# The opening of a hybrid decoder layer on one core: low parts written over their sums, a common ring of nine tiles, and the first weights split in halves

## The chip, the core and the metric

The kernel runs on one core of one Trainium2 chip. The metric is the device time of one execution in microseconds; lower is better. The core has four engines that compute (TensorE or PE, VectorE or DVE, ScalarE or ACT, GpSimd or POOL) and SyncE (SP), whose queue issues all of this kernel's DMAs. The engines run side by side and wait for one another through semaphores; each works through its own queue in order.

## What is computed

One decoder layer with two attention branches over the same input. The reference, cut to what matters:

```python
xn = rms_norm(h, norm_gain[l])                    # 16 meta tokens + 2048 tokens, 1024 wide
proj = xn @ w_in[l]                               # 1024 -> 6400 columns
sb_q, sb_k, sb_v, sw_q, sw_k, sw_v, sb_z, sw_z, g_sb, g_sw = jnp.split(proj, offsets, axis=-1)
o_sb = stick_breaking_attention(sb_q, sb_k, sb_v)          # 8 heads of 64
o_sw = sliding_window_sink_attention(rope(sw_q), rope(sw_k), sw_v, sinks)   # 16 heads, 2 k/v heads
y_sb = (o_sb * jax.nn.silu(sb_z)) @ w_branch_sb[l]
y_sw = (o_sw * jax.nn.silu(sw_z)) @ w_branch_swa[l]
merged = jax.nn.sigmoid(g_sb) * y_sb + jax.nn.sigmoid(g_sw) * y_sw
h = h + merged @ w_out[l]
return rms_norm(h, final_norm_gain)[:, BLOCK:]
```

All of it is float32. The kernel gets that accuracy by splitting each operand in a high part (`fp32r`) and a low part (what the high part leaves), and by making three products of each pair: high by high, low by high, high by low. A *split* is therefore everywhere: ScalarE writes the high part, and VectorE or GpSimd writes source minus high part.

## The kernel before

**Tiling.** Tokens lie in four groups of 512; groups 2 and 3 (`g0`, `g1` in the code of the opening) are the first half, groups 0 and 1 the second. A *column tile* is 128 columns of `w_in` for one group: 8 slices of the 1024-long contraction, three matmuls each, 24 matmuls of 128x512 (lines 402, 403, 404: xh by wh, xl by wh, xh by wl). Where the meta tokens are wanted too, 16 small matmuls of 128 columns follow (line 413, `gemm_meta`).

**The opening** (pool "start", lines 945 to 1046) begins before the norms are known. Three column tiles are wanted first: the keys of stick-breaking head pair 0 (`sb_k(0)`), the queries (`sb_q(0)`) and the keys of pair 1 (`sb_k(1)`). For both groups they are multiplied on x times gain alone (`unscaled`, lines 914 to 919), and the six sums are multiplied by the row scales afterwards (`scaled`, line 941: VectorE takes a sum from PSUM into a `tmp` tile). The sums are then split (`evac_split`, lines 112 to 114) and written to DRAM (`kd`, `qd`). Meanwhile x is normalised for good (`normal`, lines 373 to 378: VectorE multiplies by gain and scale, line 375; ScalarE writes the high part xh, line 376; VectorE writes the low part xl, line 378), first for g0, then for g1. `in_turns` does two slices at a time.

**After it** come, in this order on TensorE: the window branch's k, v and first q tile for g0 (banks g, g, z), k for g1 (bank o), v for g1 (bank z), its second q tile for g0, the stick-breaking v tile `sb_v(0)` for g1 and then g0. Rope (lines 597 to 603) takes four ScalarE copies, two VectorE operations and a GpSimd addition; `put_k` (lines 605 to 613) writes four casts and four differences into `kk`.

**Work that hangs behind a tile** is kept in three lists, `soon`, `late` and `pending`. `lagged` empties them at the third, fifth and seventh of a column tile's slices, so TensorE's order has a tile's transposes (lines 425, 471, 510, 521, 537) inside the next tile.

**Turned v.** `sb_v` makes differences of neighbouring tokens of v, and `rows` turns them: four transposes into the single bank zm (line 510), then a split into a tile `vt` of 128 x 4 x 2 x 128, which lies in the weights' `raw` buffers for g < 2 and in a buffer of its own otherwise, and one DMA per tile of v.

**Buffers.** The ring `tmp` has 7 tiles of 128x512 floats; the weights have 3 buffers each for wh and wl and 2 for `raw`; `xs` has 4. Banks in PSUM: g 2, z 2, t 2, zm 1, o 1. A buffer is free again when all that read it are done, DMAs to DRAM included.

**What sets the order.** TensorE's queue is in the order in which the code is written. ScalarE's and SyncE's queues are in written order inside the pool "start", VectorE's up to `hand.close()`; everywhere else a scheduler places instructions by a simulated time line when the program is built. The spills of split weights to DRAM (kept for the other group) are put in a list, `put_off`, in the opening.

## Time and profile before

| what | value |
|---|---|
| time, median of 3 runs | 2190.73 us (2188.23 to 2192.26) |
| time of the profiled execution | 2189.51 us |
| its span, first to last instruction | 2187.8 us |
| TensorE busy | 2153.3 us, 98% |
| VectorE busy | 1357.2 us, 62% |
| ScalarE busy | 1007.7 us, 46% |
| GpSimd busy | 370.6 us, 17% |
| mean granted clock of TensorE | 0.996 |

In a timeline row the columns are: start in us from the span's start, duration in us, engine, line, operation, what is written and what is read, shapes, the number of like instructions merged in the row, and in brackets the engine's idle time just before with the instruction that ended it. A matmul's duration has its pipeline in it, so the pace of a stream is read from the distance between starts. PE is the matmul, PEld its weight load, SPq SyncE's DMA queue. In the table by stages the columns are: the stage, its length, busy time and number of instructions for each engine, the granted clock (1.00 is full speed), the busy share of the DMA engines and GB/s.

### The profile page before, as it was taken

The numbers are of one execution on the slowest core, as the hardware profiler recorded it, in microseconds if no ns is written. First come the engines' busy times: TensorE is split into PE (matmuls) and PEld (weight loads), VectorE is DVE, ScalarE is ACT, GpSimd is POOL, SyncE is SP. The second block draws the span as 40 slices with busy tenths as digits, with TensorE's granted clock in tenths as the row PEclk, the third lists the DMA queues.
The fourth block names the chain that finished last, engine by engine and source line by source line (L and its number), as shares of the span: only waits on it lengthen the run. The fifth ranks groups of instructions, "written<-read, shape, count | busy, mean of one in ns | idle before, by whom it ended". The sixth has DMA issues, their size and how long they took to land.

```text
span 2187.8 us, 30234 instructions
## 1 busy us (share of the span) xinstructions
PE 2153.3 (98%) x10614; PEld 1768.4 (81%) x10614; DVE 1357.2 (62%) x2117; ACT 1007.7 (46%) x2327; POOL 370.6 (17%) x485
## 2 busy tenths in 40 slices
PE   8899999999999999999999999999999999999998
PEld 6678888888888888888887888888888888787886
DVE  6678776355555443777755888788774436454453
ACT  6566766244444423767753555555553301221121
POOL 1123333322322200222310000000000232000000
PEclk9899999999999999999999999999999999999999
DMA  9655544856565365444446433323323985468422
GB/s 336 236 174 182 176 174 168 275 191 199 185 194 186 125 220 164 155 154 147 143 162 190 121 111 114 113 98 114 119 86 107 353 290 189 167 221 280 154 97 87
DMA packets 174648, 380.41 MB, mean 174 GB/s; under 512 B 22912, under 2 KB 41088, under 8 KB 174496
## 3 DMA queue, kind: packets, MB, share of 16 engines
q1 hardware_dynamic: 174496, 378.48, 51.6%
q8 instruction: 84, 1.38, 0.3%
q14 instruction: 68, 0.56, 0.1%
HBM read 237.35 MB, written 140.98 MB: 173 GB/s over the span
## 4 chain that ended last, share of the span: by engine, by line
PE 88%; DVE 2%; issue 2%; ACT 2%; DMA 1%; POOL 0%; POOLq 0%; SPq 0%; ACTq 0%; DVEq 0%
PE ps_g L402 15%; PE ps_g L403 14%; PE ps_g L404 14%; PE ps_o L868 6%; PE ps_z L820 6%; PE ps_t L842 5%; PE ps_o L723 2%; PE ps_z L677 2%; PE ps_g L225 1%; PE ps_g L226 1%; PE ps_z L226 1%; PE ps_g L224 1%; PE ps_z L224 1%; PE ps_z L225 1%; PE ps_t L226 1%
## 5 line engine op out<-in xcount | busy, mean ns | idle before, releaser
L402 PE MATMUL ps_g<-xh,wh 128*128 128x512 f32 x1544 | 638.9, 414 | 7.9 <-ACT xh L918 7.5
L403 PE MATMUL ps_g<-xl,wh 128*128 128x512 f32 x1544 | 607.9, 394 | 0.5 <-DVE xl L919 0.5
L404 PE MATMUL ps_g<-xh,wl 128*128 128x512 f32 x1544 | 608.0, 394 | 0.0
L831 DVE TENSOR_TENSOR_SCAN row<-row 128x512 f32<-128x512 f32 (+2 forms) x320 | 371.2, 1162 | 167.9 <-POOL row L829 97.0
L404 PEld LDWEIGHTS ps_g<-xh,wl 128*128 128x128 f32 x1544 | 291.0, 188 | 65.6
L402 PEld LDWEIGHTS ps_g<-xh,wh 128*128 128x128 f32 x1544 | 292.5, 189 | 55.3 <-ACT xh L918 7.5
L403 PEld LDWEIGHTS ps_g<-xl,wh 128*128 128x128 f32 x1544 | 292.9, 190 | 44.1 <-DVE xl L919 1.0
L824 ACT ACTIVATE row<-ps_z 128x512 f32<-128x512 f32 (+1 forms) x320 | 171.9, 538 | 253.0 <-PE ps_z L820 208.8
L114 DVE SCALAR_TENSOR_TENSOR wtl<-ps_t,wth 128x512 fp32r<-128x512 f32 (+1 forms) x320 | 190.0, 594 | 46.7 <-ACT wth L113 45.2
L113 ACT ACTIVATE wth<-ps_t 128x512 fp32r<-128x512 f32 (+1 forms) x320 | 170.2, 532 | 91.4 <-PE ps_t L842 89.5
L820 PE MATMUL ps_z<-kt,q 128*128 128x512 f32 (+3 forms) x640 | 185.0, 369 | 0.3 <-ACT row L824 0.3
L842 PE MATMUL ps_t<-ident,row 128*128 128x128 f32 x1088 | 171.6, 273 | 1.2 <-DVE row L831 1.2
L842 PEld LDWEIGHTS ps_t<-ident,row 128*128 128x128 f32 x1088 | 135.9, 140 | 37.3 <-DVE row L831 1.7
L829 POOL TENSOR_SCALAR_AFFINE_SELECT row<-row 128x128 f32<-128x128 f32 x128 | 44.9, 352 | 620.1 <-ACT row L824 548.0
L820 PEld LDWEIGHTS ps_z<-kt,q 128*128 128x128 f32 x640 | 118.7, 188 | 26.4 <-ACT row L824 0.8
L109 POOL TENSOR_SCALAR wh<-raw 128x1024 fp32r<-128x1024 f32 (+1 forms) x63 | 66.7, 1059 | 357.6 <-PE ps_g L403 217.6
L868 PE MATMUL ps_o<-wth,vc 128*128 128x512 f32 (+1 forms) x320 | 125.7, 393 | 1.2 <-DVE tmp L873 1.1
L553 ACT ACTIVATE tmp<-ps_g 128x512 f32<-128x512 f32 x112 | 67.0, 598 | 117.5 <-PE ps_g L404 111.1
L868 PE MATMUL ps_o<-wtl,vc 128*128 128x512 f32 (+1 forms) x320 | 116.8, 365 | 0.0
L685 ACT ACTIVATE sc<-sc,nm 128x129 f32<-128x129 f32 x256 | 100.0, 393 | 36.1 <-DVE nm L683 35.4
L110 POOL TENSOR_TENSOR wl<-raw,wh 128x1024 fp32r<-128x1024 f32 (+1 forms) x43 | 95.8, 2228 | 3.2
L603 POOL TENSOR_TENSOR tmp<-tmp 128x512 f32<-128x512 f32 (+1 forms) x37 | 47.7, 1290 | 195.3 <-DMA qd<-tmp 72.2
(302 smaller groups left out, 3412.7 us busy)
## 6 DMA issues: line engine op xcount, KB each, us to landing
wh<-h_in_w_in SPq DMA_DIRECT2D x66, 512.0 KB, 4.0
wl<-l_in_w_in SPq DMA_DIRECT2D x66, 512.0 KB, 4.7
raw<-in_w_in SPq DMA_DIRECT2D x50, 512.0 KB, 5.7
h_in_w_in<-wh SPq DMA_DIRECT2D x50, 512.0 KB, 3.3
l_in_w_in<-wl SPq DMA_DIRECT2D x50, 512.0 KB, 2.9
q<-qd SPq DMA_DIRECT2D x128, 128.0 KB, 2.9
vc<-vd SPq DMA_DIRECT2D x48, 256.0 KB, 3.3
kd<-tmp SPq DMA_DIRECT2D x32, 256.0 KB, 3.8
```

What stands on the lines that cost most here:

```text
L110: (V if vsplit[0] else G).tensor_tensor(l, src, f32(h), op=ALU.subtract)
L113: A.activation(h, acc, AF.Copy, scale=scale)
L114: V.scalar_tensor_tensor(l, acc, scale, f32(h), op0=ALU.mult, op1=ALU.subtract)
L402: T.matmul(acc, lhsT=wh[:, k, :], rhs=xh[g][:, k, :], start=k == 0, stop=False)
L403: T.matmul(acc, lhsT=wh[:, k, :], rhs=xl[g][:, k, :], start=False, stop=False)
L404: T.matmul(acc, lhsT=wl[:, k, :], rhs=xh[g][:, k, :], start=False, stop=k == KT - 1)
L685: A.activation(sc[:, hh, :], sc[:, hh, :], AF.Exp, bias=nm[:, hh:hh + 1], accum_out=den[:, hh:hh + 1])
L820: T.matmul(z[:, :w], lhsT=lq, rhs=kt[h][:, k0:k0 + w], start=t == 0, stop=t == 1)
L824: A.activation(r[:, :w], z[:, :w], AF.Sigmoid, scale=-1.0)
L831: V.tensor_tensor_scan(r[:, :w], r[:, :w], r[:, :w], last[j] if n else 1.0, op0=ALU.mult, op1=ALU.min)
L842: T.transpose(tr[:, j * P:(j + 1) * P], rows_of[h, g, n - (j > i), j][:, k0:k0 + P], ident)
L868: T.matmul(o[:, :n], lhsT=v, rhs=r, start=first and r is wh, stop=last and r is wl)
```

## The change

Eight edits, all but two in the opening:

- **First weights in halves.** The weights of `sb_k(0)` are loaded first, then the gains, then x; the identity matrix is loaded later. The split is made in halves along the contraction (`by_halves`): ScalarE casts the first four slices, VectorE makes their low part; after the first slice of x, ScalarE casts the other four, and GpSimd makes their low part.
- **Low parts over sums.** In the opening `low(acc)` gives the sum's own tile as the place for its low part, so a split takes one new `tmp` tile and not two.
- **The second group's splits come earlier.** The sums of g1 are scaled and split inside the opening, before g1 is normalised; before, they were split after three column tiles.
- **Spills later.** The spills in `put_off` and the two parked sums are issued behind the splits' DMAs, the spills behind the last two loads of x.
- **The ring has 9 tiles** (7 before).
- **Turned v goes through the ring:** each tile is split in two halves (`a` = 0, 1), each 128 x 4 x 128 in a `tmp` tile, with a DMA each. The `vt` buffers go.
- **Parked sums.** The meta sums of the two key tiles come back from DRAM into the scales' tile `rb` (named `back`), both at once and earlier; the work that reads them is flushed one tile later than before. The transposed meta keys of the window branch use bank t.
- **Keys and queries held.** `put_k` and the q tile's splits for g0 are held (`then`, `waiting`) until all of the rope work of that stretch stands in VectorE's queue; `put_k` of g1 is held until the turn of v is flushed.

The core of the diff:

```diff
-        return tp.tile([rows, GT], dt, tag="tmp", name="tmp", bufs=7)
+        return tp.tile([rows, GT], dt, tag="tmp", name="tmp", bufs=9)
...
+    spare = [False]
+    def low(acc):
+        return acc.bitcast(F32R) if spare[0] else tmp(F32R)
+    sums_back = []
     def sb_k(p):
         def use(g, acc, ms):
-            h, l = tmp(F32R), tmp(F32R)
+            h, l = tmp(F32R), low(acc)
...
-                    if p < 2:
-                        t = tp.tile([NM, P], F32, tag="ms", name="ms", bufs=2)
-                        DMA(t, msd[p])
-                    mc = meta_cols(t if p < 2 else ms, "t" if p < 2 else "zm")
+                    mc = meta_cols(sums_back[p] if p < 2 else ms, "t" if p < 2 else "zm")
...
     def sb_q(p):
-            h, l = tmp(F32R), tmp(F32R)
+            h, l = tmp(F32R), low(acc)
...
-                if g < 2:
-                    vt = wp.tile([P, 4, 2, P], F32R, tag="raw", name="vt", bufs=2)
-                else:
-                    vt = tp.tile([P, 4, 2, P], F32R, tag="vt", name="vt", bufs=1)
-                evac_split(vt[:, :, :, 0:64], vt[:, :, :, 64:128], tr.rearrange("p (b a d) -> p b a d", b=4, a=2))
-                DMA(vd[p][g].rearrange("a p b d -> p b a d"), vt)
+                hl = tr.rearrange("p (b a d) -> p a b d", b=4, a=2)
+                for a in range(2):
+                    vt = tmp(F32R).rearrange("p (b d) -> p b d", b=4)
+                    evac_split(vt[:, :, 0:64], vt[:, :, 64:128], hl[:, a])
+                    DMA(vd[p][g][a], vt)
...
+    waiting = []
+    def then(f):
+        if hold[0]:
+            waiting.append(f)
+        else:
+            f()
+    hold = [False]
...
-                put_k(t, n * GT, GT)
+                then(lambda: put_k(t, n * GT, GT))
...
+        def by_halves(wh, wl, raw):
+            a, b = slice(0, KT // 2), slice(KT // 2, KT)
+            A.copy(wh[:, a], raw[:, a])
+            V.tensor_tensor(wl[:, a], raw[:, a], f32(wh[:, a]), op=ALU.subtract)
+            def rest():
+                A.copy(wh[:, b], raw[:, b])
+                G.tensor_tensor(wl[:, b], raw[:, b], f32(wh[:, b]), op=ALU.subtract)
+            second.append(rest)
+        raw = load(C_SBK)
+        DMA(gn, gain.rearrange("o (k p) -> p (o k)", p=P))
+        ready[C_SBK] = weights(C_SBK, raw=raw, split=by_halves)
...
             unscaled(g0, k, raws[k])
+            if k == 0:
+                second[0]()
         ts.append(sbt[2]())
+        DMA(ident, ident_c)
...
-        for n in (0, 2):
-            DMA(msd[n // 2], ms[n])
-        for k, t in put_off:
-            DMA(k, t)
-        del put_off[:]
         ready[C_SWQ] = weights(C_SWQ, raw=raw)
+        spare[0] = True
         outs[g0, 2] = scaled(g0, 2, rb0)
         for n in range(3):
             ts[n][1](g0, outs[g0, n], ms[n])
         for n in range(3):
             outs[g1, n] = scaled(g1, n, rb1)
-        for k, t in put_off:
-            DMA(k, t)
+        for n in range(3):
+            ts[n][1](g1, outs[g1, n], None)
+        spare[0] = False
+        for n in (0, 2):
+            DMA(msd[n // 2], ms[n])
         for k in range(0, KT, 2):
             in_turns(*(normal(g1, j, new[j], rb1) for j in (k, k + 1)))
             if k == 0:
                 for j in (6, 7):
                     new.append(ring_x())
                     DMA(new[j], xt[g1, j])
+                for j, t in put_off:
+                    DMA(j, t)
...
+                hold[0] = True
                 drain(col_tile(wk, g0, use_k), col_tile(wv, g0, use_v), col_tile(wq, g0, use_q, bank="z"))
-                for n in range(3):
-                    ts[n][1](g1, outs[g1, n], None)
+                flush(waiting)
                 drain(lagged(col_tile(wk, g1, use_k, True, "o", "t")))
+                hold[0] = False
                 meta_k = pending[:]
                 del pending[:]
                 drain(col_tile(wv, g1, use_v, True, "z", "t"))
+                pending.append(lambda: flush(waiting))
+                back = tp.tile([P, GT], F32, tag="rb", name="back", bufs=1)
+                for i in range(2):
+                    sums_back.append(back[:NM, i * P:(i + 1) * P])
+                    DMA(sums_back[i], msd[i])
...
-                pending.extend(held)
+                pending.append(lambda: pending.extend(held))
```

What this does to the queues is seen at three places. TensorE's own order stays as it was, but for three small transposes.

The first is VectorE's queue where the six sums are scaled and split. `tmp<-ps` is a sum being scaled, `tmp<-tmp` the low part of a split, `xs<-xs,gn,rb` and `raw<-raw,gn,rb` slices of x for g1 being normalised, `xl` their low parts. Before:

```order
L941 TENSOR_TENSOR tmp<-ps_z,rb_529 128x512
L114 SCALAR_TENSOR_TENSOR tmp<-tmp 128x512 x3
L941 TENSOR_TENSOR tmp<-ps_z,rb 128x512
L941 TENSOR_TENSOR tmp<-ps_o,rb 128x512
L941 TENSOR_TENSOR tmp<-ps_t,rb 128x512
L375 SCALAR_TENSOR_TENSOR xs<-xs,gn,rb 128x512 x2
L378 TENSOR_TENSOR xl<-xs,xh 128x512 x2
```

The change:

```order
L957 TENSOR_TENSOR tmp<-ps_z,rb_531 128x512
L112 SCALAR_TENSOR_TENSOR tmp<-tmp 128x512 x3
L957 TENSOR_TENSOR tmp<-ps_z,rb 128x512
L957 TENSOR_TENSOR tmp<-ps_o,rb 128x512
L957 TENSOR_TENSOR tmp<-ps_t,rb 128x512
L112 SCALAR_TENSOR_TENSOR tmp<-tmp 128x512 x3
L373 SCALAR_TENSOR_TENSOR xs<-xs,gn,rb 128x512 x2
L376 TENSOR_TENSOR xl<-xs,xh 128x512 x2
```

Three more low parts stand ahead of the normalised x; before, those three stood some fifteen rows further down.

The second place is SyncE's queue at the same point: `h_in_w_in` and `l_in_w_in` are spills of weights, `msd` the parked sums, `ct` and `sn` the rope tables, `kd` and `qd` the split sums, `xs<-in_xt` the last two slices of x for g1. Before:

```order
L55 DMA raw<-in_xt 128x512 x2
L55 DMA msd_289<-ms 16x128
L55 DMA msd_290<-ms 16x128
L55 DMA h_in_w_in_641<-wh 128x1024
L55 DMA l_in_w_in_642<-wl 128x1024
L55 DMA h_in_w_in_658<-wh 128x1024
L55 DMA l_in_w_in_659<-wl 128x1024
L55 DMA kd_2_98<-tmp 128x512 x2
L55 DMA qd_2_82<-tmp 128x512 x2
L55 DMA kd_2_102<-tmp 128x512 x2
```

The change, from the same load on:

```order
L55 DMA raw<-in_xt 128x512 x2
L55 DMA kd_2_96<-tmp 128x512 x2
L55 DMA qd_2_80<-tmp 128x512 x2
L55 DMA kd_2_100<-tmp 128x512 x2
L55 DMA ct<-in_cost 128x1024
L55 DMA sn<-in_sint 128x1024
```

and some rows on, behind the second group's split sums:

```order
L55 DMA msd_287<-ms 16x128
L55 DMA msd_288<-ms 16x128
L55 DMA xs<-in_xt 128x512 x2
L55 DMA h_in_w_in_643<-wh 128x1024
L55 DMA l_in_w_in_644<-wl 128x1024
```

Four spills of 512 KB each no longer stand ahead of the first split sums; all six stand behind the last slices of x.

The third place is the start of ScalarE's queue. Before:

```order
L65 ACT_TABLE_LOAD
L107 CAST wh<-raw 128x1024
L918 ACTIVATE xh<-raw_322,gn 128x512
L918 ACTIVATE xh<-raw_326,gn 128x512
L918 ACTIVATE xh<-raw_330,gn 128x512
```

The change:

```order
L65 ACT_TABLE_LOAD
L972 CAST wh<-raw 128x512
L934 ACTIVATE xh<-raw_321,gn 128x512
L976 CAST wh<-raw 128x512
L934 ACTIVATE xh<-raw_327,gn 128x512
```

Half of the cast now stands behind the first slice of x, and the low part of that half has moved from VectorE's queue to GpSimd's.

More of the change, by code (lines that the diff above doesn't have):

```diff
@@ L66, in tile_kernel @@
     ident = cp.tile([P, P], F32, name="ident")
-    DMA(ident, ident_c)
     gn = cp.tile([P, KT], F32, name="gn")
-    DMA(gn, gain.rearrange("o (k p) -> p (o k)", p=P))
     sel = cp.tile([P, 2, P], I32, name="sel")
@@ L163, in load, with weights @@
         return raw
-    def weights(c0, w=w_in, raw=None):
+    def weights(c0, w=w_in, raw=None, split=split):
         if c0 in ready:
@@ L626, in later @@
                         t, u = (tmp()[:, :NM] for _ in range(2))
-                        rope(meta_cols(ms), cm, sm, t, u, 1.0)
+                        rope(meta_cols(ms, "t"), cm, sm, t, u, 1.0)
                         put_k(t, 8 * P, NM)
@@ L654, in use, with put_q @@
                 q = sp.tile([P, 2, GT], F32R, tag="q", name="q", bufs=QB)
-                for a in range(2):
-                    r = slice(64 * a, 64 * a + 64)
-                    o = slice(64 - 64 * a, 128 - 64 * a)
-                    A.copy(q[r, a, :], t[r])
-                    V.tensor_tensor(q[o, a, :], t[r], f32(q[r, a, :]), op=ALU.subtract)
+                def put_q():
+                    for a in range(2):
+                        r = slice(64 * a, 64 * a + 64)
+                        o = slice(64 - 64 * a, 128 - 64 * a)
+                        A.copy(q[r, a, :], t[r])
+                        V.tensor_tensor(q[o, a, :], t[r], f32(q[r, a, :]), op=ALU.subtract)
+                then(put_q)
                 qs[p, g] = q, clock[0] + QW
@@ L951, in tile_kernel @@
             V.memset(t, 0.0)
+        second = []
+        def by_halves(wh, wl, raw):
[9 more added lines that the diff above has]
+        ready[C_SBK] = weights(C_SBK, raw=raw, split=by_halves)
         ts = [sbt[0]()]
```

## The prediction, made before the changed kernel was run

> **What bounds the kernel now.** I read the page first: the span, the busy shares and the chain of work that ended last, then its list of DMA issues.

> ```profile
> span 2187.8 us, 30234 instructions
> PE 88%; DVE 2%; issue 2%; ACT 2%; DMA 1%; POOL 0%; POOLq 0%; SPq 0%; ACTq 0%; DVEq 0%
> kd<-tmp SPq DMA_DIRECT2D x32, 256.0 KB, 3.8
> ```

> TensorE carries 88% of the chain, so a change that leaves its work alone can win only where it waits or runs at a lower clock. A table by stages shows where.

> ```profile
> 7.46:13.62 6.16, 5.65 (x13) 4.08 (x14) 5.88 (x9) 4.94 (x8) 0.00 (x0) 1.00 1.03 366
> 13.62:63.85 50.23, 50.23 (x246) 41.17 (x245) 33.59 (x64) 29.36 (x62) 8.02 (x10) 1.00 0.96 357
> 63.85:78.98 15.13, 10.25 (x45) 6.70 (x44) 12.56 (x15) 7.25 (x12) 5.38 (x3) 0.89 0.77 260
> 78.98:107.54 28.56, 23.08 (x115) 18.44 (x113) 20.04 (x36) 18.05 (x39) 5.21 (x6) 0.86 0.58 200
> 107.54:114.23 6.69, 6.69 (x27) 5.24 (x26) 0.56 (x4) 0.63 (x3) 0.00 (x0) 0.85 0.00 0
> 114.23:165.00 50.77, 47.69 (x258) 39.60 (x257) 41.07 (x79) 34.95 (x102) 14.08 (x17) 1.00 0.56 187
> 165.00:2187.80 2022.80, 2009.70 (x9922) 1653.14 (x9920) 1241.52 (x1909) 909.52 (x2100) 335.50 (x441) 1.00 0.50 168
> ```

> After 165 us it is busy for 2009.7 of 2022.8 us, and from 13.62 to 63.85 without a break. The holes lie between 63.85 and 114.23: k for g1 (third row), then v for g1, the second q tile and `sb_v(0)` for g1 (fourth), then `sb_v(0)` for g0 (fifth). To price them I need TensorE's own pace, from its timeline.

> ```profile
> 7.46 0.79 PE L402 MATMUL ps_g<-xh,wh 128*128 128x512 f32 x1 [7.46 <-ACT xh L918]
> 8.76 0.79 PE L403 MATMUL ps_g<-xl,wh 128*128 128x512 f32 x1 [0.51 <-DVE xl L919]
> 63.85 0.39 PE L402 MATMUL ps_o<-xh,wh 128*128 128x512 f32 x1
> 64.08 0.39 PE L403 MATMUL ps_o<-xl,wh 128*128 128x512 f32 x1
> 74.62 0.50 PE L403 MATMUL ps_o<-xl,wh 128*128 128x512 f32 x1 [2.21 <-DVE xl L378]
> 84.53 0.22 PE L413 MATMUL ps_t<-wh,mx 128*48 128x128 f32 x1
> 85.48 0.45 PE L402 MATMUL ps_g<-xh,wh 128*128 128x512 f32 x1
> 94.16 1.12 PE L471 MATMUL ps_zm<-ident,tmp 128*128 128x128 f32 x4 [3.69 <-ACT tmp L467]
> 94.93 0.78 PE L402 MATMUL ps_g<-xh,wh 128*128 128x512 f32 x1
> 105.02 0.20 PE L425 MATMUL ps_t<-ident,ms 16*128 16x16 f32 x1 [1.79 <-DVE q L659]
> ```

> Starts are 0.23 us apart, so a column tile of 24 matmuls takes 5.5 us; a meta product takes 0.95 (84.53 to 85.48); four transposes 0.77 (94.16 to 94.93). The third stage would take 5.5 + 0.77 + 0.95 = 7.2 without waits and takes 15.13: **8.0 lost**. The fourth would take 3 x 5.5 + 2 x 0.95 + 0.77 and some 0.4 for three small transposes = 19.6, and takes 28.56: **9.0 lost**. The fifth would take 5.6 and takes 6.69: **1.1 lost**, at a clock of 0.85.

> **The start: 0.8 us won.** TensorE begins when a weight load, its cast and one slice of x are through.

> ```profile
> 0.79 0.39 SPq L55 DMA_DIRECT2D ident<-in_ident  x1
> 1.71 0.57 SPq L55 DMA_DIRECT2D raw<-in_w_in  x1
> 5.74 1.04 ACT L107 CAST wh<-raw 128x1024 fp32r<-128x1024 f32 x1 [3.67 <-DMA raw<-in_w_in]
> 6.69 5.48 ACT L918 ACTIVATE xh<-raw,gn 128x512 fp32r<-128x512 f32 x8
> ```

> The load goes out 0.92 us earlier, so it should be seen at 4.8 and its half cast end at 5.4. Then the first slice of x decides: it is issued 0.45 earlier (the identity's slot), and was there by 6.69, so now by 6.24 at the latest; if it takes the weights' 4.03 us (5.74 less 1.71), by 5.9. TensorE's first matmul wins 0.45 to 0.8, and the second no longer waits its 0.51 for VectorE, which has half a weight tile to do. Against it, GpSimd's half of the low part (about 1.3 us, half of the 2.66 below) may hold up the second slice's low part. Bounds 0.4 and 1.3.

> **k for g1: 7.4 of 8.0 won.** What made it late stands in four queues.

> ```profile
> 48.84 2.13 DVE L114 SCALAR_TENSOR_TENSOR tmp<-tmp 128x512 fp32r<-128x512 f32 x3 [0.67 <-ACT tmp L113]
> 58.65 0.69 DVE L941 TENSOR_TENSOR tmp<-ps_o,rb 128x512 f32<-128x512 f32 x1 [6.95 <-DMA kd<-tmp]
> 59.96 0.74 DVE L375 SCALAR_TENSOR_TENSOR xs<-xs,gn,rb 128x512 f32<-128x512 f32 x1
> 52.11 3.65 SPq L55 DMA_DIRECT2D kd<-tmp  x2
> 47.42 0.80 SPq L55 DMA_DIRECT2D raw<-in_xt  x2
> 71.12 2.84 DVE L375 SCALAR_TENSOR_TENSOR xs<-xs,gn,rb 128x512 f32<-128x512 f32 x1
> 70.75 2.66 POOL L110 TENSOR_TENSOR wl<-raw,wh 128x1024 fp32r<-128x1024 f32 x1
> 51.97 2.39 POOL L110 TENSOR_TENSOR wl<-raw,wh 128x1024 fp32r<-128x1024 f32 x1
> ```

> VectorE stands for 6.95 us because the ring of seven is full until a key's DMA has landed, and that DMA stands behind four spills: it goes out at 52.11. Normalising x for g1 therefore starts at 59.96 and its last low part lets TensorE go at 74.62. In the change no scaled sum needs a ring tile that waits, and the keys' DMAs follow the x loads: out at 48.2, 0.45 apart, landing 3.8 later (the page's row). The second group's three high parts take over the tiles of the first three DMAs, so they start at about 52.0, 52.5 and 53.0; with 0.63 each on ScalarE and 0.71 each on VectorE (2.13 for three) the last low part ends at 54.3. If GpSimd's weight split (to 54.36) holds VectorE off, it ends at 56.5. I take 55.5: 4.5 us earlier than 59.96.

> From the start of normalising to the last low part it took 15.4 us (59.96 to 74.62, and 0.7 for one more low part). One slice of that took 2.84 where another took 0.74, while GpSimd made a weight's low part beside it; without that it is about 13, and GpSimd's split can't stand there in the change, since its buffers (those of k's weights) come free only after this tile. So the last low part is there at about 68.5. TensorE reaches k for g1 at 63.85 less 0.8, and its 8th slice's low part 22 matmuls and four transposes later, at 68.9. Nothing is left over; I keep 0.6 lost, from 0 (start at 54.3) to 3 (start at 57, or the last two slices of x landing late among split sums and rope tables).

> [...]

> **The three tiles after it: 6.5 of 9.0 won.** The 3.69 at 94.16 is v's copy for g1, late behind ScalarE's queue; after it the clock is below full (0.86 over the stage). Held keys and queries bring the rope and the copies forward. From the last high part of x (about 68) ScalarE has the v copy, q's rope (4 x 0.6), vv (0.6), k's rope (2.4), four casts, a sum, two q casts and v's copy: about 11 us.

> ```profile
> 79.35 2.53 ACT L611 CAST kk<-tmp 64x512 fp32r<-64x512 f32 x4
> 80.00 1.47 DVE L613 TENSOR_TENSOR kk<-tmp,kk 64x512 fp32r<-64x512 f32 x2 [3.46 <-ACT kk L611]
> 91.08 0.68 DVE L114 SCALAR_TENSOR_TENSOR vv<-ps_zm,vv 128x512 fp32r<-128x512 f32 x1
> ```

> That is 79, and TensorE wants the copy at 63.05 + 0.6 + 7.2 (k) + 6.5 (v) + 4.8 (seven slices of q) = 82. But bank zm must also be free, and its last reader on VectorE (the 0.68) now stands behind k's four differences and q's two, which end at 80 to 81 and, with GpSimd's split of the second q weights beside them, up to 2.4 later. So it is close here, and again one tile on, at `sb_v(0)`'s meta product and its transpose: three places, 0 to 1.5 us each; I take 0.8, 0.7 and 1.0. Bounds of what is lost: 0 and 5.

> [...] Here the pause of 1.79 at 105.02 was followed by a clock of 0.85. [...]

> **The rest: 2.5 won.** Without the pause the fifth stage's 1.1 goes (0 to 1.1). Two transposes wait on turned v.

> ```profile
> 126.47 0.27 PE L521 MATMUL ps_zm<-ident,vf 128*8 128x128 f32 x1 [1.06 <-DVE vt L114]
> 160.26 0.27 PE L521 MATMUL ps_zm<-ident,vf 128*8 128x128 f32 x1 [1.63 <-DVE vt L114]
> L113 ACT ACTIVATE vt<-ps_zm x16: 581/598/602, 117.2 to 1106.2; 128x512 fp32r<-128x512 f32 x16
> L114 DVE SCALAR_TENSOR_TENSOR vt<-ps_zm,vt x16: 669/682/692, 117.8 to 1106.8; 128x512 fp32r<-128x512 f32 x16
> 128.12 0.41 ACT L699 CAST xs<-tmp 128x256 fp32r<-128x256 f32 x1
> ```

> The splits now come ahead of the next rope in ScalarE's queue; I take half of 2.7 (0 to 2.7). Sixteen turned tiles cost two operations of about 0.41 each instead of one of 0.6 to 0.68 on each engine, some 3 us of ScalarE and of VectorE in all, under TensorE, which is busy 99% after 165 us while VectorE is busy 61%; if that cover went, at most those 3 us. The 16 more DMA issues and the few rows that the scheduler turned round in the second half count nothing, give or take 1.5.

> **Sum.** 0.8 + 7.4 + 6.5 + 1.1 + 1.4 = 17.2 us off the profiled 2189.5 (span 2187.8 and 1.7 around it): 2172.3. The median of the runs is 1.2 above the profiled one, so **2173.5**. All bounds at their best give 22; at their worst, 0.4 + 5 + 4 = 9.4.

> **Rivals.** *VectorE becomes the bound of 64 to 114 us.* It was busy 12.56 + 20.04 us in two stages that shrink from 43.7 to about 30; without the moved splits and GpSimd's hindrance some 28 us of work stay, 93%. For: it hands over to ScalarE at each split and idles meanwhile. Against: it stood nearly idle (0.56 of 6.69) right after. If it gets no denser than 80%, the stages last 35: 5 lost, some 3 more at half clock; gain 9, 2182. *The wait only moves.* If the first keys' DMAs land not 3.8 but 9 us after issue (the x loads and rope tables share the queues), the high parts come at 57 and normalising starts at 59.5 as before; what stays is the start and turned v, 2 us: 2188.5. *The ring stalls elsewhere.* Turned v now holds up to four ring tiles until its DMAs have landed, and rope, gates and the next turn queue behind it. If each of 16 turned tiles made TensorE wait the 1.63 of the row above, 26 us would go and the kernel take 9 longer, 2200; from 17 / 16 = 1.1 us each it is slower. Against: nine tiles, and a DMA of half the size.

> **Chances.** The forecast 0.64, VectorE as the bound 0.22, the moved wait 0.08, the ring 0.06. A measurement tells 0.2%, 4.4 us, from no change. Faster by more: the first two cases and a little of the third, 0.88; same: the rest of the third and a little of the fourth, 0.07; slower: the rest of the fourth, 0.05. Range 2168.5 to 2183.5: best bounds to a little beyond the second case.

> **What will show it.** VectorE's 6.95 on `kd` gone and normalising of g1 begun near 55; TensorE's first matmul near 6.8; no 3.69 at line 471's successor; `sb_v(0)`'s meta product for g1 ending near 93 rather than 107.54. I am wrong if TensorE still waits on xl for g1 for more than 3 us in all, if the granted clock stays under 0.9 between 64 and 100 us, or if waits on the ring appear after 165 us.

## The result, and the profile after

The changed kernel takes 2175.93 us (median of four runs, 2175.12 to 2176.53), the kernel before 2190.91: a ratio of 0.9932, interval 0.9916 to 0.9948. The forecast was 2173.5, with 2168.5 to 2183.5. The sums below are made between the two profiled executions, 2189.51 and 2175.12 us: 14.4 us won where the prediction's sum says 17.2.

From the page of the changed kernel, its span and its row of keys' DMAs:

```profile
span 2173.4 us, 30334 instructions
kd<-tmp SPq DMA_DIRECT2D x32, 256.0 KB, 4.8
```

The table by stages of the changed kernel, cut at the same instructions as the prediction's table (the start and its 50.23 us stage are one row here). Columns: length, then busy time and instructions of TensorE, its weight loads, VectorE, ScalarE and GpSimd, then the granted clock, the DMA share and GB/s.

```profile
6.77:62.69 55.92, 55.48 (x257) 44.20 (x258) 45.79 (x80) 38.06 (x75) 9.10 (x11) 1.00 0.96 349
62.69:70.94 8.25, 7.44 (x45) 5.62 (x44) 6.46 (x10) 5.21 (x9) 0.75 (x1) 1.00 1.03 396
70.94:92.94 22.00, 20.17 (x113) 15.57 (x111) 16.14 (x22) 14.34 (x29) 9.25 (x6) 1.00 0.75 267
92.94:99.56 6.62, 6.11 (x27) 4.78 (x28) 4.04 (x15) 3.51 (x12) 1.57 (x3) 1.00 0.50 198
99.56:148.17 48.61, 47.39 (x259) 39.75 (x257) 39.51 (x81) 34.54 (x104) 16.03 (x17) 1.00 0.58 197
148.17:2173.40 2025.23, 2010.70 (x9922) 1654.03 (x9920) 1246.64 (x1923) 911.75 (x2114) 335.57 (x441) 1.00 0.50 168
```

k for g1 takes 8.25 us instead of 15.13, the three tiles after it 22.00 instead of 28.56, and the granted clock is full in every row where it was 0.89, 0.86 and 0.85. But the fifth stage takes 6.62, hardly less than the 6.69 of before, although its clock is full now, and the last row takes 2.43 more than before. Set side by side, the start of the same TensorE instruction in the two traces, and what is won up to it:

```
instruction                                  before    after     won   in between
first matmul                                   7.46     6.77    0.69
transposes of rb for g1                       47.06    45.90    1.16   start: 1.16
first matmul of v for g1                      78.98    70.94    8.04   k for g1: 6.88
first matmul of sb_v(0) for g0               107.54    92.94   14.60   three tiles: 6.56
end of the fifth stage                       114.23    99.56   14.67   fifth stage: 0.07
around 165 us                                165.00   148.17   16.83   turned v: 2.16
end of the span                             2187.80  2173.40   14.40   the rest: -2.43
```

Where an expectation below speaks of 7 us for the three tiles, it counts to the end of the meta product before that first matmul, at 92.07, and so leaves out the wait of 0.85 between the two.

TensorE's timeline shows the waits of 0.2 us and more that are left in the opening, save two of 0.40 and 0.39 (in brackets the wait and what ended it; the second row is there for its 0.40, the first at full clock):

```profile
6.77 0.80 PE L400 MATMUL ps_g<-xh,wh 128*128 128x512 f32 x1 [6.77 <-ACT xh L934]
10.95 0.40 PE L402 MATMUL ps_g<-xh,wl 128*128 128x512 f32 x1
67.52 0.50 PE L400 MATMUL ps_o<-xh,wh 128*128 128x512 f32 x1 [0.59 <-ACT xh L374]
68.24 0.50 PE L401 MATMUL ps_o<-xl,wh 128*128 128x512 f32 x1 [0.22 <-DVE xl L376]
82.83 0.63 PE L474 MATMUL ps_zm<-ident,tmp 128*128 128x128 f32 x4 [0.35 <-DVE vv L112]
85.25 0.51 PE L402 MATMUL ps_g<-xh,wl 128*128 128x512 f32 x1 [0.64 <-DVE wl L108]
92.94 0.50 PE L400 MATMUL ps_g<-xh,wh 128*128 128x512 f32 x1 [0.85 <-DVE tmp L614]
98.72 0.23 PE L423 MATMUL ps_zm<-ident,ms 16*128 16x16 f32 x1 [0.51 <-DVE ms L418]
110.59 0.27 PE L523 MATMUL ps_zm<-ident,vf 128*8 128x128 f32 x1
137.44 0.63 PE L513 MATMUL ps_zm<-ident,tmp 128*128 128x128 f32 x4 [1.22 <-DVE tmp L112]
```

Nothing over 1.3 us is left after the first row. The gaps in TensorE's timeline over the whole span, the one before its first matmul among them, add up to 27.2 us before and 18.8 now, so 8.4 of the 14.4 are waits. The other 6.0 go with the clock. The kernel before ran at half clock in three stretches of 13.64 us in all, 11.92 of them busy, which is about 6.0 lost (a table by windows laid on them; the granted clock is the number behind GpSimd's):

```profile
75.37:78.78 3.41, 3.41 (x20) 2.98 (x21) 1.17 (x2) 2.83 (x5) 1.27 (x1) 0.50 0.56 183
92.44:99.26 6.82, 5.10 (x14) 4.22 (x15) 4.57 (x7) 4.73 (x9) 1.27 (x1) 0.50 0.65 222
106.09:109.50 3.41, 3.41 (x22) 3.03 (x20) 1.34 (x5) 1.19 (x5) 0.00 (x0) 0.50 0.05 5
```

In the changed kernel the clock is full from 10.7 us on.

VectorE's timeline of the changed kernel, with GpSimd's split and one row of ScalarE's beside it, shows the queue that made k for g1 late:

```profile
48.37 1.87 DVE L112 SCALAR_TENSOR_TENSOR tmp<-tmp 128x512 fp32r<-128x512 f32 x3
52.75 1.96 DVE L112 SCALAR_TENSOR_TENSOR tmp<-tmp 128x512 fp32r<-128x512 f32 x1 [0.70 <-ACT tmp L111]
56.03 1.41 DVE L373 SCALAR_TENSOR_TENSOR xs<-xs,gn,rb 128x512 f32<-128x512 f32 x2
51.77 2.40 POOL L108 TENSOR_TENSOR wl<-raw,wh 128x1024 fp32r<-128x1024 f32 x1
54.00 1.39 ACT L111 ACTIVATE tmp<-tmp 128x512 fp32r<-128x512 f32 x2 [1.28 <-DMA kd<-tmp]
```

The 6.95 on `kd` is gone and normalising of g1 begins at 56.03 (55.5 was forecast, 59.96 stood before). One difference took 1.96 beside GpSimd's 2.40, where three took 1.87 without it. A wait on the landing of a key is left, 1.28 us on ScalarE, ahead of the second group's high parts.

### The profile page after: what moved, and what is told of

Read it like the earlier page. It is cut to its first block, busy times and chain, and to the rows that moved or that the text cites. A ratio compares the mean times of both kernels' runs of the same rounds, so it can differ in the third digit from the quotient of the medians.

```text
span 2173.4 us, 30334 instructions
## 1 busy us (share of the span) xinstructions
PE 2147.3 (99%) x10614; PEld 1764.0 (81%) x10614; DVE 1360.6 (63%) x2133; ACT 1010.1 (46%) x2344; POOL 374.7 (17%) x486
## 5 line engine op out<-in xcount | busy, mean ns | idle before, releaser
L402 PE MATMUL ps_g<-xh,wl 128*128 128x512 f32 x1544 | 607.5, 393 | 1.0 <-DVE wl L108 1.0
L402 PEld LDWEIGHTS ps_g<-xh,wl 128*128 128x128 f32 x1544 | 290.3, 188 | 66.9 <-DVE wl L108 1.9
L401 PEld LDWEIGHTS ps_g<-xl,wh 128*128 128x128 f32 x1544 | 292.0, 189 | 43.7 <-DVE xl L935 1.3
L107 POOL TENSOR_SCALAR wh<-raw 128x1024 fp32r<-128x1024 f32 (+1 forms) x63 | 65.8, 1045 | 331.3 <-PE ps_g L401 142.8
## 6 DMA issues: line engine op xcount, KB each, us to landing
vc<-vd SPq DMA_DIRECT2D x48, 256.0 KB, 3.9
kd<-tmp SPq DMA_DIRECT2D x32, 256.0 KB, 4.8
```

The costliest lines, as they stand in the source:

```text
L401: T.matmul(acc, lhsT=wh[:, k, :], rhs=xl[g][:, k, :], start=False, stop=False)
L402: T.matmul(acc, lhsT=wl[:, k, :], rhs=xh[g][:, k, :], start=False, stop=k == KT - 1)
```

## The experiments

Twelve more runs were made, in four groups, each beside the kernel before on the same chip (medians there 2189.07 to 2189.82). The ratio to it is what is compared; the changed kernel run once more gave 0.9932 again. Medians are compared within a group or with that second run, 2173.91. Where two intervals overlap, only the traces tell the kernels apart.

> The changed kernel as it is, beside the others of this call: 2174 to 2176, ratio 0.993.

Measured: 2173.91 us, 0.9932 (0.9919 to 0.9946). From 15 to 1566 us its trace stays within 0.4 us of the first one (at 12 us it is 0.9 away, as full clock came at 12.3 and not at 10.7); then it is 0.5 behind at 1716 and 1.2 ahead at 2016. So about a microsecond there differs from one execution of the same kernel to the next.

### Nine tiles alone

```diff
 (the kernel before)
-        return tp.tile([rows, GT], dt, tag="tmp", name="tmp", bufs=7)
+        return tp.tile([rows, GT], dt, tag="tmp", name="tmp", bufs=9)
-                if g < 2: vt = wp.tile(...) else: vt = tp.tile(...)
-                evac_split(vt[:, :, :, 0:64], vt[:, :, :, 64:128], ...)
+                for a in range(2):
+                    vt = tmp(F32R).rearrange("p (b d) -> p b d", b=4)
+                    evac_split(vt[:, :, 0:64], vt[:, :, 64:128], hl[:, a])
```

> The kernel before with one part of the change: turned v goes in two halves through the common ring, and the ring has nine tiles; start, sums, order of the splits and the DMAs stay as before. Theory (a full ring of seven is what VectorE's 6.95 us on kd are): with nine tiles the three scaled sums of g1 take over the tiles of the first sums, which are split by then, so the 6.95 goes, normalising of g1 starts near 53 instead of 59.96, and k for g1 wins 6 to 7 of its 8.0 lost us; the 3.69 of v's copy and the rest of the three tiles after it stay, turned v wins about 2. Sum 8 to 9: 2182 (2180 to 2184). Rival (the ring alone does nothing for k, since the next tile it hands out waits for the same landing; low parts in place and the keys' DMAs behind the x loads are needed): VectorE still stands 4 us or more on kd, only turned v's 2 us come: 2189.

Measured: 2184.76, 0.9982 (0.9973 to 0.9991). Its table by windows (k for g1, then the three tiles, cut at the same instructions) and three rows of TensorE's and ScalarE's timelines:

```profile
64.27:71.13 6.86, 6.86 (x45) 5.79 (x44) 4.15 (x6) 4.78 (x8) 0.89 (x1) 1.00 0.89 305
71.13:104.57 33.44, 24.28 (x114) 19.28 (x113) 22.90 (x36) 18.54 (x40) 11.40 (x9) 0.83 0.60 218
```

```profile
87.58 1.12 PE L471 MATMUL ps_zm<-ident,tmp 128*128 128x128 f32 x4 [4.96 <-ACT tmp L467]
101.23 0.26 PE L425 MATMUL ps_t<-ident,ms 16*128 16x16 f32 x1 [4.16 <-DMA ms<-msd]
81.66 0.62 ACT L657 CAST q<-tmp 64x512 fp32r<-64x512 f32 x1 [6.63 <-POOL tmp L602]
```

k for g1 runs in 6.86 us without a wait: 8.27 us won there, by this run's one edit, in which the ring is what the theory named. Normalising of g1 starts at 52.87. The theory holds for it, and low parts over sums and the new order of the DMAs are not needed for it. Whether those two would do it with seven tiles was not run. But the next row takes 33.44 where it took 28.56: 4.9 are given back. TensorE is 7.9 us sooner at v's transposes and v's copy only 6.6: ScalarE stood 6.63 us for a rope sum of GpSimd (the third row) and made the copy behind that. Then a transpose waits 4.16 for the load that brings a parked meta sum back. Turned v wins 1.5 (from 2.71 at 118 us to 4.21 at 190).

The same load explains the 1.79 at 105.02 in the kernel before, which its profile puts down to VectorE's q. There the view of the tile `msd` has the second load go out at 103.3, behind the transpose at 103.00 that frees the buffer:

```profile
L55 SPq DMA_DIRECT2D ms<-msd x2: 307/312/318, 101.5 to 103.3; - x2
```

The trace has the load's last piece at 104.89, 0.1 us before the transpose's weights are read. VectorE's operation on q ends at 104.94, but the transpose doesn't use q.

### Three parts of the change taken back, one at a time

```diff
 (a_nolow)     -        return acc.bitcast(F32R) if spare[0] else tmp(F32R)
               +        return tmp(F32R)
 (a_nohold)    -                hold[0] = True
 (a_oldstart)  identity and gain first, no by_halves, no second[0]()
```

> The changed kernel, but the low parts take ring tiles of their own and do not overwrite the sums. Theory (the nine tiles do the work): the scaled sums of g1 find the tiles of the first sums free, the second group's splits wait for the six keys' and queries' DMAs about as they wait for three now, normalising of g1 starts within 1 us of 56.03, time within 1 us of 2175.9. Rival (low parts over sums are what frees VectorE): normalising of g1 starts 2 us or more later, TensorE waits for it at 68, where only 0.8 of slack is left: 2179 to 2183.

> The changed kernel, but keys and queries are put in place at once and not held back. Theory: ScalarE then has k's four casts (2.5 us) ahead of k's rope for g1 and of v's high part, and VectorE its differences ahead of the one that frees bank zm; the wait of 0.35 before v's transposes for g1 and the 0.64 on the low part of the weights behind them grow to 1 to 3 us, time 2177 to 2179. Rival (the queues have room there, holding back is worth nothing): within 0.7 us of 2175.9.

> The changed kernel with the start as before: identity and gain loaded ahead of the first weights, the first weights cast and split whole. Theory: TensorE starts near 7.46 instead of 6.77, is 1.16 us later at 46 us, and nothing behind it takes that up: 2177.1 (2176.5 to 2177.6). Rival (TensorE waits for later loads anyway, the 0.40 on the second weights at 15.63 and the last low parts of x at 68 take it up): within 0.4 us of 2175.9. What would blur it: the clock is granted in steps of 3.41 us, and full speed began at 10.74 in the changed kernel and at 13.93 before; by another position of that step the same start is worth up to 1.6 more or less.

Measured: 2174.08, 0.9933 (0.9919 to 0.9946); 2174.55, 0.9933 (0.9921 to 0.9946); 2174.78, 0.9935 (0.9922 to 0.9947). None can be told from the changed kernel.

Low parts over sums: worth nothing with nine tiles, as the theory said. Without them normalising of g1 starts at 55.80.

Holding back: the expectation of 1 to 3 us fails. v's transposes do wait longer, but the two waits behind them go:

```profile
83.78 0.63 PE L474 MATMUL ps_zm<-ident,tmp 128*128 128x128 f32 x4 [1.97 <-DVE vv L112]
92.84 0.50 PE L400 MATMUL ps_g<-xh,wh 128*128 128x512 f32 x1 [0.79 <-DVE tmp L614]
```

1.97 and 0.79 here, 0.35, 0.64, 0.85 and 0.51 in the changed kernel: 2.8 against 2.4 us.

The start: with the old one TensorE begins at 7.47 and stands 0.55 us behind at 60 us, but only 0.22 behind at 215, since in the tiles up to 100 us it waits less (0.48, 0.84 and 0.47 where 0.35, 0.64, 0.85 and 0.51 stood). The rival is nearer the truth: more than half of what the start wins is taken up by shorter waits for VectorE behind it, and the 0.2 that stays is less than the runs can tell.

### The second group's splits late again, then without holding back too

```diff
 (a_late)
         for n in range(3):
             outs[g1, n] = scaled(g1, n, rb1)
-        for n in range(3):
-            ts[n][1](g1, outs[g1, n], None)
         spare[0] = False
 ...
                 flush(waiting)
+                spare[0] = True
+                for n in range(3):
+                    ts[n][1](g1, outs[g1, n], None)
+                spare[0] = False
                 drain(lagged(col_tile(wk, g1, use_k, True, "o", "t")))
 (late_nohold)  a_late, and
-                hold[0] = True
```

> The changed kernel, but the second group's sums are split where they were before: behind the three column tiles of g0 and not ahead of the normalising of g1. Theory (the 7 us of the three tiles come from this move, since the run with nine tiles alone won 8.3 us at k for g1 and then waited 4.96 on v's copy and 4.16 on a meta sum): k for g1 still runs without a long wait, one or both of these waits come back with half clock behind them, 2181 to 2185. Rival (they come from holding keys and queries back and from the parked sums): within 1.5 us of the changed kernel's time.

> The changed kernel with both taken back: the second group's sums are split behind the three column tiles of g0, and keys and queries are put in place at once. Either alone cost nothing (2173.3 and 2174.6). Theory E (either of the two is enough to keep ScalarE's queue ahead of v's copy for g1 short, and only without both does the wait come back): v's copy waits 3 to 5 us, half clock follows, 2179 to 2182. Rival D (what the three tiles won lies elsewhere, in the parked meta sums and in the order of the loads and spills, which the run with nine tiles alone also lacked): no wait over 2 us between 75 and 100, 2173 to 2175.5.

Measured: 2173.31, 0.9925 (0.9911 to 0.9938), and 2175.67, 0.9937 (0.9924 to 0.9951). Splitting early wins nothing; split late, the kernel is 2.0 us ahead of the changed one in the trace at 113 us. The first 1.3 of that come at x for g1, where TensorE's two waits (0.59 and 0.22) are gone since its normalising starts at 51.93 and not at 56.03. Without both, v's transposes wait:

```profile
84.10 1.05 PE L474 MATMUL ps_zm<-ident,tmp 128*128 128x128 f32 x4 [2.78 <-DVE vv L112]
```

That and the half clock behind it put it 4.2 us behind late splits alone at 89 us; 2.2 come back at bank g, where late splits alone wait 2.01. So 2.0 us are lost, where E looked for 5 to 8. Both theories are off: either part does spare a wait, as E has it, but it carries some 2 us of the three tiles' 6.6, and the rest lies elsewhere, as D has it.

### The parked meta sums as before

```diff
 (the changed kernel)
-                    mc = meta_cols(sums_back[p] if p < 2 else ms, ...)
+                    if p < 2:
+                        t = tp.tile([NM, P], F32, tag="ms", name="ms", bufs=2)
+                        DMA(t, msd[p])
+                    mc = meta_cols(t if p < 2 else ms, ...)
-                back = tp.tile([P, GT], F32, tag="rb", name="back", bufs=1)
-                ...  DMA(sums_back[i], msd[i])
-                pending.append(lambda: pending.extend(held))
+                pending.extend(held)
-                        rope(meta_cols(ms, "t"), cm, sm, t, u, 1.0)
+                        rope(meta_cols(ms), cm, sm, t, u, 1.0)
```

> The changed kernel with the parked meta sums as before: each is read back into the two-buffered tile of the meta sums when its transpose is due, not ahead of time into the scales' tile, the meta work that was kept back comes one place earlier, and the rope of k's sum uses bank zm. Theory M (of the 7 us that the three tiles won, the part that neither early splits nor holding back brought is this read-back: in the run with nine tiles alone the second such transpose waits 4.16 us on the load of ms at 101.23, and the 1.79 at 105.02 of the kernel before stands at the same transpose): that transpose waits 1.8 to 4.2 us again, half clock may follow it, 2 to 6 us lost, 2176 to 2180. Rival (with the rest of the change the tile comes free early enough and the load lands in time): no wait over 0.7 there, within 1 us of 2174 to 2176.

Measured: 2181.70, 0.9964 (0.9950 to 0.9977). Theory M holds, and beyond its high end: 0.6 us ahead of the changed kernel at 85 us, 6.9 behind it at 100. Three rows of TensorE's timeline, one of SyncE's queue, the times from issue to landing of the DMAs that touch `msd`, and the window behind them:

```profile
90.31 0.23 PE L423 MATMUL ps_zm<-ident,ms 16*128 16x16 f32 x1 [2.42 <-DVE vv L112]
93.55 0.28 PE L423 MATMUL ps_t<-ident,ms 16*128 16x16 f32 x1 [1.18 <-DMA ms<-msd]
96.20 0.26 PE L423 MATMUL ps_t<-ident,ms 16*128 16x16 f32 x1 [2.37 <-ACT kk L627]
88.14 0.32 SPq L55 DMA_DIRECT2D ms<-msd  x1
DMA to landing us min/median/max: 4.9/5.4/5.5
```

```profile
91.72:101.96 10.24, 6.70 (x29) 5.02 (x28) 4.57 (x14) 3.86 (x15) 1.53 (x3) 0.50 0.39 146
```

The loads go out when the two-buffered tile is free, the first at 88.14, the next 2.4 us later, and land some 5.4 us after that, near 93.5 and 96.1. So the second and the third transpose both wait for a load, though the profile names ScalarE for the third: the trace has the last piece of its load at 96.06. In the changed kernel, SyncE's queue has both at 70.30, into the scales' tile, which nobody else wants:

```profile
70.30 1.80 SPq L55 DMA_DIRECT2D back<-msd  x2
```

Against 1.36 us of waits in the changed kernel between 86 and 100 there are 5.97 here, 4.6 more; the other 2.9 of the 7.5 are half clock, under which TensorE worked for 6.70 us. Two of the three waits, 3.55 us, are for the loads. The first, 2.42, is at the transpose of k's meta sum, which this edit puts back into bank zm, and `vv`, that bank's last reader, ends it. Which line of the edit does most wasn't tried apart.

### Turned v in one piece, and what can be had on top

```diff
 (a_wholev)
-                for a in range(2):
-                    vt = tmp(F32R).rearrange("p (b d) -> p b d", b=4)
-                    evac_split(vt[:, :, 0:64], vt[:, :, 64:128], hl[:, a])
-                    DMA(vd[p][g][a], vt)
+                h, l = tmp(F32R), tmp(F32R)
+                evac_split(h, l, tr)
+                for i, t in enumerate((h, l)):
+                    DMA(vd[p][g].rearrange("a p b d -> p b a d")[:, :, :, 64 * i:64 * i + 64],
+                        t.rearrange("p (b a d) -> p b a d", b=4, a=2))
 (late_wholev)     a_wholev and a_late together
 (late_wholev_vs)  late_wholev, and vsplit[0] = True where C_SWQ and the next query
                   weights are split: VectorE makes their low parts, not GpSimd
```

> The changed kernel, but turned v is split in one piece: the high parts of both halves go to one ring tile, the low parts to another, one operation each on ScalarE and VectorE; the two DMAs then write runs of 256 bytes and not 512. Theory (the 1.22 at 137.44 comes from the two halves standing apart in ScalarE's queue, the first at 132.81, the second behind four exponentials at 136.30, so that bank zm is kept 5.4 us): that wait and the 0.39 behind it go, 1.0 to 1.6 us won, 16 fewer operations on each of the two engines change nothing. Rival (the bank was kept by the ring's landing, or shorter DMA runs bring new waits): no gain, or up to 1 us lost.

> The changed kernel with two edits: the second group's sums split late, as in the run that did this alone (2.0 us ahead of the changed kernel at 215 us), and turned v split in one piece (1.5 ahead at 215 us). Theory (the two lie at different places and add up): no wait left at the transposes of turned v near 135, 3 to 4 us faster than the changed kernel, 2170 to 2171. Rival (the two meet in the same queues, as the split sums and turned v share the ring): no better than the better of the two, 2172 to 2173.5.

> As the run with both edits, and the low parts of the first two query weights are made by VectorE (1.2 us each) and not by GpSimd (2.4 and 2.85). [...]

Measured: 2172.52, 0.9923 (0.9910 to 0.9935); 2169.92, 0.9912 (0.9899 to 0.9926); 2168.66, 0.9906 (0.9892 to 0.9919). In one piece, the wait at turned v shrinks and 1.6 us are won between 128 and 158 us, as forecast:

```profile
136.50 0.66 PE L513 MATMUL ps_zm<-ident,tmp 128*128 128x128 f32 x4 [0.26 <-DVE tmp L112]
```

In the changed kernel the two halves stand apart on ScalarE, with four exponentials between them, and bank zm is kept meanwhile:

```profile
132.81 0.37 ACT L111 ACTIVATE tmp<-ps_zm 128x256 fp32r<-128x256 f32 x1
136.30 0.39 ACT L111 ACTIVATE tmp<-ps_zm 128x256 fp32r<-128x256 f32 x1
```

With late splits too, the gains add up by the medians, but in the traces 2.6 us are left at 215 us of 2.0 and 1.5. The wait of 2.01 on bank g stands in both kernels with late splits; with v in one piece as well it lies in one step of the clock (explained in the next experiment) that has TensorE busy for 0.41, and half clock follows it, which it doesn't in late splits alone. With the low parts moved to VectorE, its four differences of k take half the time; from VectorE's and GpSimd's timelines with late splits alone, and VectorE's of the last kernel:

```profile
70.37 7.03 DVE L626 TENSOR_TENSOR kk<-tmp,kk 64x512 fp32r<-64x512 f32 x4 [1.06 <-ACT kk L624]
72.55 2.85 POOL L108 TENSOR_TENSOR wl<-raw,wh 128x1024 fp32r<-128x1024 f32 x1
```

```profile
73.60 3.53 DVE L626 TENSOR_TENSOR kk<-tmp,kk 64x512 fp32r<-64x512 f32 x4
```

And the table by windows of the last kernel, over the three tiles, cut at the same instructions:

```profile
70.03:90.47 20.44, 19.45 (x112) 15.76 (x110) 17.54 (x23) 14.65 (x30) 6.59 (x5) 1.00 0.99 360
```

VectorE is busy for 17.54 of 20.44 us there, 86%, and TensorE waits only once for it, 0.99. This kernel is 5.2 us under the changed kernel by the medians, 4.8 in the traces at 188 us. Against the kernel without the last edit it is 1.3 by the medians, with intervals that overlap, and 2.2 in the traces, of which 1.6 are the half clock that no longer follows bank g. The two moved splits take 1.23 and 2.31 us on VectorE, so with the 3.53 of the differences its own time stays the same, 7.1 us where the differences alone took 7.0. It is the version to keep.

### Pauses of a known size

```diff
 (the changed kernel, in the gates' use, for 21 column tiles of the first half)
+                t = tmp()
+                A.copy(t, src)
+                for _ in range(n):
+                    G.tensor_copy(t, t)
+                tr = ps("t")
+                T.transpose(tr[:, :P], t[:, :P], ident)
```

> The changed kernel with 21 pauses put into TensorE's work while the gates of the first half run: after a column tile a copy of its sum by ScalarE, 0 to 4 copies of that by GpSimd, and a transpose that waits for them, so that TensorE stands about 1.0, 1.6, 2.2, 2.8 or 3.4 us; of seven, three each are single pauses of each of these five lengths and three each are pairs (1.0 + 1.0 and 1.6 + 1.6) with 0.7 us of matmuls between. Theory W (the clock is set anew every 3.41 us and falls to half after a step in which TensorE was busy less than about half, as the steps of the kernel before with shares of 0.35, 0.42, 0.48 and 0.49 did and those with 0.55 and 0.67 did not): no drop after a single pause under 1.7, a drop after every one of 3.4 and after most between, and after pairs of 1.6. [...] Rival L (a single pause over 1.7 us is always followed by half clock): every 2.2 drops, no pair does.

Measured: 2278.62 us, with 27 pauses of 0.7 to 4.8 us. (The longest was planned at 3.4, so the sizes are read from the trace.) In every trace the clock changes only at multiples of 3.41 us from its first change (in the kernel before, full clock comes at 13.93 and the first half clock at 75.37, 61.44 us or 18 steps on). A table with windows on such steps, each followed by the next (length, TensorE's busy time and matmuls, granted clock):

```profile
425.50:428.91 3.41, 1.59 (x7) 1.00 0.28 108
428.92:432.33 3.41, 2.54 (x15) 1.00 0.20 77
818.04:821.45 3.41, 1.57 (x8) 1.00 0.20 77
821.46:824.86 3.40, 3.40 (x12) 0.50 0.00 0
753.18:756.59 3.41, 1.75 (x11) 1.00 0.21 77
756.60:760.00 3.40, 3.40 (x20) 1.00 0.00 0
473.29:476.70 3.41, 2.70 (x10) 0.50 0.00 0
476.71:480.11 3.40, 3.40 (x10) 0.50 0.00 0
497.18:500.59 3.41, 2.85 (x8) 0.50 0.53 191
500.60:504.00 3.40, 3.40 (x20) 1.00 0.01 2
```

One pause of 2.70 lay across two steps (first pair of rows) and had no half clock behind it; neither had one of 2.51 (third pair). Two pauses of 1.16 and 0.68 fell into one step (second pair), and the clock fell. Theory W holds, L falls. Laid over all traces of this case, up to TensorE's last work: of the steps at full clock, every one of the 22 in which TensorE was busy for 0.46 or less is followed by half clock, one of three between 0.47 and 0.48, and none of those from 0.49 up. At half clock the next step is full again after a share of 0.84 or more (23 of 23) and stays at half up to 0.79 (12 of 12). So 1.84 us of pauses in one step sufficed for half clock behind it (second pair).

## Why the prediction was right, and where not

The time came out inside the range and 2.4 us over the forecast, on the side that holds most of the chance. By its steps:

- **The start, 0.8.** Mis-sized twice. In the trace 1.16 is won at 46 us, more than the first matmul's 0.69; full clock came at 10.7 and not at 13.9, 3.2 sooner, which also hangs on how the steps of 3.41 us lie. But the old start put back costs 0.55 us at 60 us, 0.22 at 215 and nothing that the medians can tell. The step that failed is to add it to the sum as if nothing behind it took it up.
- **k for g1, 7.4 of 8.0.** 6.88 measured, with normalising from 56.03 (55.5 said). That VectorE stood because of a ring of seven is shown: nine tiles alone win 8.27. That is more than the 8.0 held to be lost, since the prediction took the pace of four transposes, 0.77, from a row at half clock; in the changed kernel at full clock they take 0.38. That low parts over sums and the keys' DMAs behind the loads of x were needed for it is wrong: the ring alone does it without either, and the low parts taken back change nothing. With the early splits a wait of 1.28 for a key's landing came back, on ScalarE, and late splits start normalising 4.1 us sooner.
- **The three tiles after it, 6.5 of 9.0.** 6.56 measured: the sum is right by luck and its reason mostly is not. The step says held keys and queries and the moved splits bring v's copy forward. Each alone is worth nothing, both together some 2 us. The parked meta sums carry most of it: put back, they cost 7.5 with the half clock behind their waits, 3.55 of it for the loads and 2.42 for bank zm. The prediction doesn't price them at all. v's wait is 4.96 with nine tiles alone and 2.78 with late splits and without holding back; what else in the change shortens it stays open. The prediction quoted the 1.79 at 105.02 with VectorE's q as the releaser; that transpose reads a parked sum, and with nine tiles alone, where the wait is 4.16, the trace names the load. As shown with that run, a load explains the 1.79 too.
- **The fifth stage, 1.1 won.** 0.07. The half clock did go, but the stage takes 6.62 and not 5.6: a meta sum's transpose waits 0.51 in it, and two small transposes (0.29) stand in it that stood in the three tiles before. At the three close places 0.8 + 0.7 + 1.0 were allowed; bank zm took 0.35, the meta product nothing and its transpose those 0.51. The low part of `sb_v(0)`'s weights (0.64) and bank g (0.85) were not among the three. In all that is 2.35 against 2.5, at other places.
- **Turned v, 1.4.** 2.16 up to 165 us, and 0.67 lost right after, where a value product waits 0.39 for GpSimd's `cl`; 1.5 in all, as with nine tiles alone: right. The 1.06 and 1.63 are gone wholly, and a new 1.22 stands against them, since the halves part on ScalarE.
- **The rest, 0 give or take 1.5.** 2.43 lost. 0.67 is that value product; 0.85 and 0.64 fell at 1862 and 1962 us, where the same kernel run again stood up to 1.2 better.

Of the 2.8 us between 17.2 and 14.4, the fifth stage is 1.03 and the rest 2.43; start, k, the three tiles and turned v together come to 0.66 more than forecast. **The rivals.** VectorE did not become the bound: the 80% that it was not to get beyond in that rival were passed in the last kernel, at 86% with one wait. The wait on the keys' landing did not move as a whole: 1.28 us on ScalarE are left of VectorE's 6.95, though the keys land 4.8 us after issue (the page's row) and not 3.8. The ring did not stall after 165 us; turned v's new wait is an order on ScalarE, and in one piece with as many ring tiles 0.26 of it is left. **Half clock behind a pause** was weighed by one row alone, and the sum gives the waits that stay their own time only. The traces bear the row out (the step with the 1.79, from 102.68 to 106.08, has TensorE busy for 0.47 and is followed by half clock), and 6.0 of the 14.4 us are half clock.

## What to carry to other kernels

A part of a change that seems to carry a gain should be taken back alone, and then with its neighbours: here two of the three parts in the title (low parts over sums, the first weights in halves) are worth nothing that could be measured, the early splits and the holding back nothing singly, and a small part, meta sums read back 18 us earlier into a tile of their own with the bank and the place that go with it, costs half of all that was won when it is taken back. When a wait goes, look at what the next one behind it reads, not only at the releaser that the profile names; a load into a tile with two buffers waits for its last reader first (in the kernel before it went out at 103.3, behind the transpose at 103.00). And count waits by the 3.41-us steps in which the clock changed here: 1.16 and 0.68 us in one step had half clock behind them, some 1.7 us more by an estimate (half of the 3.40 that TensorE was busy there), and 2.70 us across two steps had none.
